# Low parts of the keys stacked over 128 rows in the attention scores of 64-row heads

## The chip, the cores and the metric

One core of one Trainium2 chip runs the whole program in one launch. The metric is the device time of that core in microseconds, as the median of three runs. Engines are named as in the profile: PE is TensorE (its matmuls; PEld its weight loads), DVE is VectorE, ACT is ScalarE, POOL is GpSimd, SP is SyncE, which issues the DMAs.

## The reference

For 512 tokens of width 2048, two hybrid attention layers run one after another, and behind them a block with a pooling branch, a state space branch and a gated embedding. The change lies in the attention of the two layers. Each layer has three branches with causal softmax attention:

```
# differential attention: 4 heads, 2 score maps each, 64 channels per map
s = einsum('bqhcd,bkhcd->bhcqk', q, k) * 64 ** -0.5      # causal mask, softmax
a = p[:, :, 0] - lam * p[:, :, 1]
# sliding window: 16 query heads, 2 key heads of 64 channels, window 128
s = einsum('bnqgrd,bnkgd->bngrqk', q, k_band) * 64 ** -0.5
# latent attention: 4 heads; 128 channels without rotation, 64 rotated, the rotated key shared
s = einsum('bqhd,bkhd->bhqk', concat(q_nope, q_rope), concat(k_nope, k_rope)) * 192 ** -0.5
```

All arrays are float32.

## The kernel before

TensorE works on float32r operands. To keep float32 accuracy every operand is split into a high part (rounded to float32r) and a low part (the rest), and a product is three matmuls into one PSUM bank: high by high, high by low, low by high (`mm3`). A matmul takes stationary weights, loaded into the array (128 rows are the channels that are summed over, 128 columns), and moves up to 512 columns of the other operand through it; every matmul has its own weight load.

The program is a sequence of projections on TensorE (512 output columns over 16 tiles of channels). The weights stream in by DMA in pieces of two units (`wraw`); ScalarE makes the high part (`whi`), VectorE the low part (`wlo`), and a ring keeps four units split ahead of the one in use (`AHEAD`). Between the steps of a projection the attention work of finished heads is placed: `step` counts the TensorE time of the projection, and each 1310 ns of it `tick` lets waiting pieces go on when a small model, kept while the program is written, finds their operands written and their banks free. So each engine has a fixed order, in which attention pieces stand between projection steps. An attention unit has five pieces: scores (TensorE, then the mask and the maximum on VectorE), exp (ScalarE), norm (VectorE), transposes (TensorE, split by ScalarE and VectorE), and probabilities times values (TensorE).

For heads of 64 channels the scores use the 128 rows of the array for two parts at once. `to_stack` takes a rotated [channel, token] tile that holds two heads, one in rows 0 to 63 and one in rows 64 to 127. For queries it makes two tiles `sa` and `sb`, one per head, with the head's high part in one half of the rows and its low part in the other (the half that has to change rows is copied by DMA). For keys of the differential branch it makes `sa` and `sb` with the head's high part in both halves, and one tile `sl` with the low parts of both heads, each in its own half. `mm_stacked` then needs two steps per score map: over 128 rows (high by high and low by high at once), and over the 64 rows in which the head's own high query part lies (high query by low key). The sliding-window keys (`hi`, `lo` from `kd`) and the latent branch's rotated key (`hi`, `lo` from `kr`) have their low part in both halves of the rows already.

In a sliding-window unit (`sw_unit`, 8 per key head and layer) two pairs of heads are worked on, each over 256 key columns, into the banks `s0` and `s1`. In a differential unit (`da_units`) the two score maps of a head go to `s0` and `s1`, over 256, 256, 384 and 512 key columns for the four query tiles. In a latent unit (`mla_units`) one head goes to one bank: three steps of `mm3` for the 128 channels, then the two stacked steps.

In the rows of the trace a matmul is written out<-moving,stationary: `s<-hi,sa` is a score step with key tile `hi` moving and the queries `sa` stationary, `s<-lo,sa` is the step with the low key tile. The helper that records every operation gives all of them line L166, so the rows are told apart by their tiles and shapes: `128*128 128x256` is a full step of 256 columns, `64*128 64x256` a step over 64 rows.

Of the kernel before, what the change touches and what calls it, by code (L numbers as in the profile page):

```python
# [85 lines left out]
class Model:  # L86
    """A rough account, kept while the program is written, of when each engine gets to an instruction and
    each tile is written. Work beside the projections is placed where its operands should be there."""
# [53 lines left out]
    def ready(self, need, eng, banks):  # L142
        """Whether eng would find these tiles written and banks of these tags free."""
        limit = max(self.t[eng], self.t["PE"])
        for tag in set(banks):
            names, bufs = self.held.get(tag, ()), self.bufs.get(tag, 1)
            for i in range(len(names) + banks.count(tag) - bufs):
                if self.used.get(names[i], 0.0) + 130 > limit:
                    return False
        return all(x is not None and self.done.get(x.tensor.name, 1e18) + 130 <= limit for x in need)  # L150
# [5 lines left out]
class Engine:  # L156
    """An engine's instructions, passed on and entered in the model."""
# [24 lines left out]
class Step:  # L182
    """A piece of work that is best begun when eng would find the tiles that need() names written."""
# [9 lines left out]
class K:  # L193
# [87 lines left out]
    def chain(self, fs, gap=1.0, delay=0.0, q=None):  # L281
        """Steps that run one after another, at least gap ticks apart; None leaves a place free, and one
        that returns False is called again later."""
        self.n += 1
        heapq.heappush(self.bg if q is None else q, (self.now + delay + gap, self.n, list(fs), gap))

    def force(self, q):
        """Runs the next step that can be, ready or not."""
        self.run_urgent()
        late, got = [], False  # L290
        while q and not got:
            x = heapq.heappop(q)
            got = self.is_emitted(x[2][0]) and self.run_step(x[2][0]) is not False
            if got:
                self.advance(q, x)
            else:
                late.append(x)
        assert got
        for x in late:
            heapq.heappush(q, x)  # L300
# [17 lines left out]
    def att_start(self, units, ticks, delay=0, done=None):  # L318
        """Units of (scores, exp, norm, transposes, values); one is begun every so many ticks."""
        gap = ticks / len(units)  # L320
        t = self.now + delay
        for x in units:
            self.queue.append([list(x), 0, t])
            t += gap
        if done:
            self.queue[-1][0].append(done)

    def run_units(self, force=False):
        """A unit goes on once the one before it is two parts further."""
        before = 5  # L330
        for x in list(self.queue):
            steps, pos, t = x
            if t > self.now and not force:
                break
            while pos < len(steps) and (before >= min(pos + 2, 5)):
                f = steps[pos]
                if not (self.is_emitted(f) if force else self.is_ready(f)):
                    break
                self.run_step(f)
                pos += 1  # L340
                if force:
                    force = False
                    x[1] = pos
                    if pos == len(steps):
                        self.queue.remove(x)
                    return True
            x[1] = pos
            if pos == len(steps):
                self.queue.remove(x)
                before = 5  # L350
            else:
                before = pos
        return False
# [18 lines left out]
    def rsqrt_list(self, out, ss, scale, eps, n):  # L372
        """Closures that put (ss * scale + eps) ** -0.5 into out[0]."""
# [26 lines left out]
    def rsqrt1(self, ss, scale, eps):  # L400
        """(ss * scale + eps) ** -0.5 of one column; the powers of two that the steps leave are taken out at the end."""
# [18 lines left out]
    def units(self, name):  # L420
        """How many units of up to 512 columns, and the k-tiles and columns of each."""
# [10 lines left out]
    def plan_loads(self):  # L432
        """Pieces of one or two units, and after which split the load of each is issued."""
# [55 lines left out]
    def ahead(self, n=AHEAD):  # L489
        """Keeps n units of the ring split beside the one in use."""  # L490
# [20 lines left out]
    def proj_cm(self, name, mov, ncol, evac, hook=None):  # L511
        """out[channel, token]: the weights stationary."""
# [17 lines left out]
    def proj_tm(self, name, stat, ms, evac, hook=None):  # L530
        """out[token, channel]: the activations stationary."""
# [99 lines left out]
    def reduce_list(self, tiles):  # L631
        """The steps of reduce_angle as closures."""
        return [lambda x=x: self.reduce_angle(*tiles(), part=x) for x in range(4)]

    def reduce_angle(self, a, k, r, part=None):
        """r = a - 2 pi round(a / 2 pi), the multiple taken off in pieces that are exact; in one go or by part."""
# [48 lines left out]
    def norm_list(self, m, xt, after_sq=None, tags="tttt", act=False, first=False):  # L685
        """Closures: x / rms(x), transposed into the columns of token tile m of B."""
# [72 lines left out]
    def rope_lists(self, raws, fins):  # L759
        """Rotates the [channel, token] tiles; fins get each result."""  # L760
# [29 lines left out]
    def to_stack(self, dst, i, keys=False):  # L790
        """Two heads of 64 rows for products whose 128 rows carry both parts: [hi; lo] and [lo; hi] of them, or,
        for keys, [hi; hi] of either, and the two heads' lo."""
        def f(x):
            a, b, lo = (self.u(F32R, name=n) for n in ("sa", "sb", "sl"))
            self.nc.scalar.copy(a, x)
            self.nc.scalar.copy(b[64:128, :], x[64:128, :])
            self.urgent.append(lambda: self.nc.vector.tensor_tensor(out=lo, in0=x, in1=a, op=ALU.subtract))

            def move():
                self.nc.sync.dma_start(a[64:128, :].bitcast(F32), (a if keys else lo)[0:64, :].bitcast(F32))  # L800
                self.nc.sync.dma_start(b[0:64, :].bitcast(F32), (b if keys else lo)[64:128, :].bitcast(F32))
                dst[i] = (a, b, lo) if keys else (a, b)

            self.chain([Step(move, lambda: [lo], "SP")], 0.3)
        return f

    def mm_stacked(self, outs, qs, ks, rows, start=True):
        """hi hi + lo hi over 128 rows, then hi lo over the head's own 64."""
# [3 lines left out]
        for o, q, k, r in zip(outs, qs, ks, rows):  # L812
            nc.tensor.matmul(o, q[r], k[1][r], start=False, stop=True)

# [1 line left out]
    def sw_unit(self, l, g, pp2, i, q, kd, v, yr):  # L816
# [8 lines left out]
        def scores():  # L825
            p, mx = [], self.small(4, name="mx")
            banks = [self.bank(f"s{e}") for e in range(2)]
            for a in range(2):
                self.mm_stacked([b[:, a * 256:(a + 1) * 256] for b in banks],
                                [x[:, i * P:(i + 1) * P] for x in q[2 * pp2 + a]],  # L830
                                [[x[:, k0 * P:k0 * P + 256] for x in kd[g]]] * 2, HALVES)
# [94 lines left out]
    def da_units(self, l, h, qk, va, done):  # L926
        """qk() gives the tiles of q and k; done(o) comes after the last one."""
# [4 lines left out]
        for i in range(NT):  # L932
# [3 lines left out]
            def scores(i=i, st=st):  # L936
# [5 lines left out]
                                [(x[:, :w], k[2][:, :w]) for x in k[:2]], HALVES)  # L942
# [33 lines left out]
    def mla_units(self, h, qk, vc, done):  # L976
# [5 lines left out]
        for i in range(NT):  # L982
# [3 lines left out]
            def scores(i=i, st=st, n=n):  # L986
# [5 lines left out]
                self.mm_stacked([b[:, :w]], [qr[e][:, i * P:(i + 1) * P]], [[x[:, :w] for x in kr]], HALVES[e:e + 1], False)  # L992
# [30 lines left out]
    def cm_norm_list(self, xs, n, eps, cols, after):  # L1023
        """Closures: x * rsqrt(mean over the channels) * column, for [channel, token] tiles, in place."""
# [60 lines left out]
    def plan_tail(self, name, last):  # L1085
        """The last chunk stays on the chip, split; the end of it stays in the ring."""
# [6 lines left out]
    def layer(self, l):  # L1093
# [66 lines left out]
        # sliding window  # L1160
# [44 lines left out]
        # differential attention  # L1205
# [47 lines left out]
        # latent attention, over the last projection and the first chunk of the output projection  # L1253
# [25 lines left out]
        def hook(k0):  # L1279
            """Rows of B that the last projection has passed take the branches' outputs."""  # L1280
# [27 lines left out]
    def tail_rows(self, name, evac):  # L1308
        """The resident last chunk, token tile by token tile."""
# [70 lines left out]
    def cmul(self, dst, a, b, e1, e2, tmp, neg_im=False):  # L1380
        """dst = a * b for (re, im) pairs of views; tmp: two scratch views."""
# [12 lines left out]
    def exp_list(self, get):  # L1394
        """exp of get() = (x, out, k, t), in closures; x, k and t are overwritten."""
# [157 lines left out]
    def cdiag(self, c, pr):  # L1553
        """c of two groups, each in its rows and columns."""
        return self.cd[c][pr // 16][:, pr % 16].rearrange("p e c -> p (e c)")

    def ssm_lists(self, ct, ud, yd, put):
        """Closures of one channel tile (8 groups): its tables, then the scan and its output."""
# [226 lines left out]
    def second(self, xsrc):  # L1785
# [36 lines left out]
        # pooling branch  # L1822
# [84 lines left out]
        # gated linear unit of the state space branch  # L1907
# [29 lines left out]
        # output projection, residual  # L1937
# [49 lines left out]
        # embedding, its gate, final norm  # L1987
# [81 lines left out]
def _layout(inp):  # L2069
# [80 lines left out]
    # constants of the shapes  # L2150
# [35 lines left out]
```

## Time and profile before

| | before |
|---|---|
| median of 3 runs | 2713.55 us (2711.83 to 2714.47) |
| profiled execution, first to last instruction (the page gives no other time for it) | 2711.1 us |
| TensorE busy | 2648.9 us, 13120 matmuls |
| TensorE weight loads busy | 2201.1 us |
| VectorE busy | 1599.1 us |
| ScalarE busy | 1197.8 us |
| GpSimd busy | 415.5 us |

The span is the time from the first to the last instruction in one execution; the median is of other executions and is 2.4 us above it. Busy is the time covered by an engine's instructions; matmuls are pipelined, so that their durations overlap, and the distance from one start to the next tells more than a duration.

### The profile page before, as it was taken

How to read it: one execution, taken by the hardware profiler on the slowest of the kernel's cores; microseconds unless marked ns; L12 is line 12 of the kernel's file. 1: busy time of each engine (PE TensorE's matmuls, PEld its weight loads, DVE VectorE, ACT ScalarE, POOL GpSimd, SP SyncE). 2: the span in 40 equal slices, each digit the busy share in tenths (PEclk: the TensorE clock that was granted, in tenths of full speed). 3: DMA queues.
4: the chain of work that ended last, by engine and by line, in shares of the span. 5: the costliest groups of instructions: out<-in, count | busy, mean ns of one | idle time of the engine just before them, and what ended most of it. 6: DMA issues, size and time to landing. Idle time of an engine off the chain costs nothing. (4 is left out here: it accounts for less than half of the span.)

```text
span 2711.1 us, 36803 instructions
## 1 busy us (share of the span) xinstructions
PE 2648.9 (98%) x13120; PEld 2201.1 (81%) x13120; DVE 1599.1 (59%) x3247; ACT 1197.8 (44%) x2543; POOL 415.5 (15%) x822
## 2 busy tenths in 40 slices
PE   8999999999999999999999999989999999999998
PEld 8978888877888887888777788888877888888886
DVE  6785566675624758546667562486767654333344
ACT  7565444544434646444444443463333343232341
POOL 0100001100001110000110000117777800000000
PEclk9999999999999999999999999999999999999999
DMA  6642333223235553224422323454232332352332
GB/s 213 186 120 86 91 119 113 75 78 125 71 116 163 173 147 94 94 89 122 117 71 79 124 70 117 160 186 141 84 94 82 100 99 94 118 164 69 101 127 91
DMA packets 125831, 309.04 MB, mean 114 GB/s; under 512 B 33616, under 2 KB 34512, under 8 KB 125648
## 3 DMA queue, kind: packets, MB, share of 16 engines
q1 hardware_dynamic: 125648, 306.69, 36.1%
q8 instruction: 103, 1.69, 0.3%
q14 instruction: 80, 0.66, 0.1%
HBM read 264.68 MB, written 20.97 MB: 105 GB/s over the span
## 5 line engine op out<-in xcount | busy, mean ns | idle before, releaser
L166 PE MATMUL pp<-B,whi 128*128 128x512 f32 (+1 forms) x4256 | 1222.6, 373 | 7.5 <-DVE g L166 6.2
L166 PEld LDWEIGHTS pp<-B,whi 128*128 128x128 f32 x4256 | 753.9, 190 | 137.7 <-issue 7.1
L166 PE MATMUL pp<-B,wlo 128*128 128x512 f32 (+1 forms) x2128 | 782.4, 368 | 8.9 <-DVE wlo L166 8.9
L166 PE MATMUL pp<-whi,B 128*128 128x512 f32 x1984 | 626.0, 391 | 1.6 <-ACT raw L166 1.0
L166 DVE SCALAR_TENSOR_TENSOR wlo<-wraw,p_cols,whi 128x512 fp32r<-128x512 f32 (+1 forms) x576 | 448.4, 795 | 293.7 <-ACT whi L166 290.0
L166 ACT ACTIVATE whi<-wraw,p_cols 128x512 fp32r<-128x512 f32 (+1 forms) x576 | 395.9, 713 | 206.8 <-PE pp L166 170.8
L166 PEld LDWEIGHTS pp<-B,wlo 128*128 128x128 f32 x2128 | 403.5, 190 | 78.2 <-DVE wlo L166 10.3
L166 PEld LDWEIGHTS pp<-whi,B 128*128 128x128 f32 x1984 | 372.4, 188 | 82.2 <-ACT raw L166 1.8
L166 DVE TENSOR_TENSOR wlo<-wraw,whi 128x512 fp32r<-128x512 f32 x288 | 197.8, 696 | 386.9 <-ACT whi L166 386.5
L166 PE MATMUL pp<-wlo,B 128*128 128x512 f32 x992 | 386.2, 389 | 0.0
L166 ACT CAST whi<-wraw 128x512 fp32r<-128x512 f32 x288 | 175.5, 623 | 323.4 <-PE pp L166 311.0
L166 PEld LDWEIGHTS pp<-wlo,B 128*128 128x128 f32 x992 | 186.4, 188 | 37.1
L166 POOL TENSOR_TENSOR sw<-sw,sinT 128x512 f32<-128x512 f32 x40 | 55.2, 1386 | 764.7 <-DMA sw<-raw 708.8
L166 POOL TENSOR_TENSOR o<-o,x 128x512 f32<-128x512 f32 x32 | 51.1, 1623 | 378.4 <-DVE o L166 370.4
L166 PE MATMUL pp<-rh,B 128*128 128x512 f32 x320 | 103.1, 392 | 0.0
L166 PE MATMUL pp<-hi,whi 128*128 128x512 f32 x224 | 88.3, 394 | 1.4 <-DVE lo L166 1.4
L166 PE MATMUL pp<-hi,wlo 128*128 128x512 f32 x224 | 87.3, 390 | 0.0
L166 PE MATMUL pp<-lo,whi 128*128 128x512 f32 x224 | 87.3, 390 | 0.0
L166 ACT ACTIVATE p<-p,nb 128x256 f32<-128x256 f32 (+1 forms) x128 | 60.2, 473 | 57.9 <-DVE nb L166 57.8
L166 ACT CAST pth<-t 128x256 fp32r<-128x256 f32 (+1 forms) x96 | 29.2, 339 | 113.2 <-PE t L166 110.5
L166 PEld LDWEIGHTS pp<-rh,B 128*128 128x128 f32 x320 | 60.1, 188 | 12.3
L166 DVE TENSOR_SCALAR p<-p,sm 128x128 f32<-128x128 f32 (+1 forms) x192 | 66.0, 386 | 4.1 <-DVE sm L166 0.5
(257 smaller groups left out, 3162.7 us busy)
## 6 DMA issues: line engine op xcount, KB each, us to landing
wraw<-in_w SPq DMA_DIRECT2D x426, 512.0 KB, 3.5
sw<-raw SPq DMA_DIRECT2D x160, 64.0 KB, 2.0
wraw<-in_w SPq DMA_DIRECT2D x24, 384.0 KB, 3.2
x<-in_x SPq DMA_DIRECT2D x32, 256.0 KB, 5.2
x<-o SPq DMA_DIRECT2D x32, 256.0 KB, 2.6
ybd<-yb SPq DMA_DIRECT2D x16, 256.0 KB, 4.5
yb<-ybd SPq DMA_DIRECT2D x16, 256.0 KB, 3.8
x<-x SPq DMA_DIRECT2D x16, 256.0 KB, 4.4
```

The costliest lines, as they stand in the source:

```text
L166: r = f(*a, **k)
```

## The change

`to_stack` for keys: the low parts of the two heads go to two tiles, `lo` and `lb`, by two subtractions over 64 rows each, and each is copied by DMA to the other half of its rows. `mm_stacked` then takes all 128 rows in the second step too, with the same stationary queries as in the first; the step now adds the product of the two low parts, which was left out before. The two steps of one score map follow each other directly, where before the first steps of both maps came ahead of the second steps. For the sliding window and the latent branch nothing but the rows and the order of the steps changes.

```
     def to_stack(self, dst, i, keys=False):
...
         def f(x):
             a, b, lo = (self.u(F32R, name=n) for n in ("sa", "sb", "sl"))
+            V = self.nc.vector
             self.nc.scalar.copy(a, x)
             self.nc.scalar.copy(b[64:128, :], x[64:128, :])
-            self.urgent.append(lambda: self.nc.vector.tensor_tensor(out=lo, in0=x, in1=a, op=ALU.subtract))
+            if keys:
+                lb = self.u(F32R, name="sl")
+                for d, r in zip((lo, lb), HALVES):
+                    self.urgent.append(lambda d=d, r=r: V.tensor_tensor(out=d[r, :], in0=x[r, :], in1=a[r, :],
+                                                                        op=ALU.subtract))
+            else:
+                self.urgent.append(lambda: V.tensor_tensor(out=lo, in0=x, in1=a, op=ALU.subtract))
 
             def move():
-                self.nc.sync.dma_start(a[64:128, :].bitcast(F32), (a if keys else lo)[0:64, :].bitcast(F32))
-                self.nc.sync.dma_start(b[0:64, :].bitcast(F32), (b if keys else lo)[64:128, :].bitcast(F32))
-                dst[i] = (a, b, lo) if keys else (a, b)
-
-            self.chain([Step(move, lambda: [lo], "SP")], 0.3)
+                dup = [(a, a if keys else lo, 0), (b, b if keys else lo, 1)] + ([(lo, lo, 0), (lb, lb, 1)] if keys else [])
+                for d, s, h in dup:
+                    self.nc.sync.dma_start(d[HALVES[1 - h], :].bitcast(F32), s[HALVES[h], :].bitcast(F32))
+                dst[i] = (a, b, lo, lb) if keys else (a, b)
+
+            self.chain([Step(move, lambda: [lo, lb] if keys else [lo], "SP")], 0.3)
         return f
 
-    def mm_stacked(self, outs, qs, ks, rows, start=True):
+    def mm_stacked(self, outs, qs, ks, start=True):
         nc = self.nc
         for o, q, k in zip(outs, qs, ks):
             nc.tensor.matmul(o, q, k[0], start=start, stop=False)
-        for o, q, k, r in zip(outs, qs, ks, rows):
-            nc.tensor.matmul(o, q[r], k[1][r], start=False, stop=True)
+            nc.tensor.matmul(o, q, k[1], start=False, stop=True)
...
-                                [[x[:, k0 * P:k0 * P + 256] for x in kd[g]]] * 2, HALVES)
+                                [[x[:, k0 * P:k0 * P + 256] for x in kd[g]]] * 2)
...
-                                [(x[:, :w], k[2][:, :w]) for x in k[:2]], HALVES)
+                                [[x[:, :w] for x in k[e::2]] for e in range(2)])
...
-                self.mm_stacked([b[:, :w]], [qr[e][:, i * P:(i + 1) * P]], [[x[:, :w] for x in kr]], HALVES[e:e + 1], False)
+                self.mm_stacked([b[:, :w]], [qr[e][:, i * P:(i + 1) * P]], [[x[:, :w] for x in kr]], False)
```

On TensorE, in the first sliding-window unit of layer one, the difference of the two programs reads as follows (`s_1779` and `s_1780` are the two score banks, `hi_1690` and `lo_1691` the keys, `sa` and `sb` the queries of the two heads of a pair; the shape is that of the columns written, so that a step over 64 rows reads as 128x256 too):

```order
 L166 MATMUL s_1779<-hi_1690,sa_1561 128x256
+L166 MATMUL s_1779<-lo_1691,sa_1561 128x256
 L166 MATMUL s_1780<-hi_1690,sb_1562 128x256
-L166 MATMUL s_1779<-lo_1691,sa_1561 128x256
 L166 MATMUL s_1780<-lo_1691,sb_1562 128x256
 L166 MATMUL s_1779<-hi_1690,sa_1612 128x256
+L166 MATMUL s_1779<-lo_1691,sa_1612 128x256
 L166 MATMUL s_1780<-hi_1690,sb_1613 128x256
-L166 MATMUL s_1779<-lo_1691,sa_1612 128x256
 L166 MATMUL s_1780<-lo_1691,sb_1613 128x256
```

Each low step moved up by one place, behind the high step into the same bank; the number of steps is the same.

On SP, where the first two key tiles of the differential branch in layer one are moved, the queue has before the change (64x512 are copies between halves of rows, `wraw` the loads of weights):

```order
L166 DMA sa_3768<-sl_3770 64x512
L166 DMA sb_3769<-sl_3770 64x512
L166 DMA wraw_3830<-in_w 128x1024
L166 DMA sa_3806<-sa_3806 64x512
L166 DMA sb_3807<-sb_3807 64x512
L166 DMA wraw_3873<-in_w 128x1024
L166 DMA sa_3841<-sa_3841 64x512
L166 DMA sb_3842<-sb_3842 64x512
L166 DMA wraw_3950<-in_w 128x1024
```

and after it:

```order
L166 DMA sb_3769<-sl_3770 64x512
L166 DMA wraw_3832<-in_w 128x1024
L166 DMA sa_3806<-sa_3806 64x512
L166 DMA sb_3807<-sb_3807 64x512
L166 DMA sl_3808<-sl_3808 64x512
L166 DMA sl_3811<-sl_3811 64x512
L166 DMA wraw_3879<-in_w 128x1024
L166 DMA sa_3845<-sa_3845 64x512
L166 DMA sb_3846<-sb_3846 64x512
L166 DMA sl_3847<-sl_3847 64x512
L166 DMA sl_3850<-sl_3850 64x512
```

Two copies of a low tile stand ahead of the next load of weights that was behind the tile's two other copies before.

## Rows read from the trace of the kernel before

**Rows 1.** The page: span, busy time and share of two engines, granted clock by slices.

```profile
span 2711.1 us, 36803 instructions
PE 2648.9 (98%) x13120; PEld 2201.1 (81%) x13120; DVE 1599.1 (59%) x3247; ACT 1197.8 (44%) x2543; POOL 415.5 (15%) x822
PEclk9999999999999999999999999999999999999999
```

**Rows 2.** Waits of TensorE, whole run: us in total, times, longest.

```profile
PE t L166 <- DVE p L166: 5.0, 5, 1.8
```

**Rows 3.** Timeline of PE, first sliding-window unit: start us, duration us, engine, line, operation, tiles.

```profile
138.65 0.28 PE L166 MATMUL s<-hi,sa 128*128 128x256 f32 x1
138.76 0.28 PE L166 MATMUL s<-hi,sb 128*128 128x256 f32 x1
138.98 0.38 PE L166 MATMUL s<-lo,sa 64*128 64x256 f32 x1
138.98 0.38 PE L166 MATMUL s<-lo,sb 64*128 64x256 f32 x1
139.29 0.38 PE L166 MATMUL s<-hi,sa 128*128 128x256 f32 x1
139.51 0.28 PE L166 MATMUL s<-hi,sb 128*128 128x256 f32 x1
...
140.03 0.73 PE L166 MATMUL pp<-B,whi 128*128 128x512 f32 x2
140.60 0.40 PE L166 MATMUL pp<-B,wlo 128*128 128x512 f32 x1
140.83 0.62 PE L166 MATMUL pp<-B,whi 128*128 128x512 f32 x2
141.29 0.39 PE L166 MATMUL pp<-B,wlo 128*128 128x512 f32 x1
```

**Rows 4.** Timeline of PE, a differential unit of 512 key columns.

```profile
426.12 0.39 PE L166 MATMUL s<-sa,sa 128*128 128x512 f32 x1
426.35 0.39 PE L166 MATMUL s<-sb,sb 128*128 128x512 f32 x1
426.67 0.50 PE L166 MATMUL s<-sl,sa 64*128 64x512 f32 x1
...
427.10 0.73 PE L166 MATMUL pp<-B,whi 128*128 128x512 f32 x2
```

**Rows 5.** Timeline of PE, end of a latent unit of 256 key columns.

```profile
643.65 0.28 PE L166 MATMUL s<-hi,lo 128*128 128x256 f32 x1
643.76 0.28 PE L166 MATMUL s<-hi,sa 128*128 128x256 f32 x1
643.97 0.38 PE L166 MATMUL s<-lo,sa 64*128 64x256 f32 x1
644.28 0.72 PE L166 MATMUL pp<-B,whi 128*128 128x512 f32 x2
```

**Rows 6.** Timeline of PE, probabilities times values of a differential head, full steps only.

```profile
407.39 0.28 PE L166 MATMUL t<-pth,hi 128*128 128x256 f32 x1
...
407.99 0.28 PE L166 MATMUL t<-pth,lo 128*128 128x256 f32 x1
408.11 0.63 PE L166 MATMUL pp<-B,whi 128*128 128x512 f32 x2
408.58 0.39 PE L166 MATMUL pp<-B,wlo 128*128 128x512 f32 x1
```

**Rows 7.** Steps on query tile sa: ns min/median/max, first and last start us, forms.

```profile
L166 PE MATMUL s<-lo,sa x80: 379/381/498, 139.0 to 1582.4; 64*128 64x256 f32 x72, 64*128 64x384 f32 x4, 64*128 64x512 f32 x4
L166 PE MATMUL s<-sl,sa x32: 379/408/500, 389.4 to 1462.7; 64*128 64x256 f32 x16, 64*128 64x384 f32 x8, 64*128 64x512 f32 x8
```

**Rows 8.** Tile sa: the subtractions that read it, and SP's issue of its copies.

```profile
L166 DVE TENSOR_TENSOR sl<-raw,sa x36: 682/692/1809, 114.6 to 1510.4; 128x512 fp32r<-128x512 f32 x36
L166 SPq DMA_DIRECT2D sa<-sa x8: 461/462/467, 358.2 to 1344.4; - x8
```

**Rows 9.** DMA issues: tiles, count, KB each, us from issue to landing.

```profile
sa<-sa SPq DMA_DIRECT2D x8, 128.0 KB, 4.3
```

## Prediction

> **What bounds the kernel now.** I read the page first. TensorE is busy 98% of the span of 2711.1 us, at full granted clock in all 40 slices [rows 1]: 2.4 GHz, the upper of its two levels. VectorE has 59% [rows 1]. A busy share of 98% says only that matmul durations cover the span; they overlap (a matmul of 512 columns lasts 0.39 us and its follower starts 0.23 us after it), so it does not say that the array streams all that time. Hence the second view, the waits. Over the whole run TensorE's transposes wait five times for VectorE's probabilities, 5.0 us together [rows 2], and span less busy time leaves 62 us without any work. A stage that shortens TensorE's own stream therefore shortens the run almost one for one, if the waits do not grow.
>
> The third view is what the change is about: the timeline of TensorE inside one score block, read by the distance from one start to the next. In a sliding-window unit [rows 3] two 128-row score steps start 0.11 us apart (138.65, 138.76). The first 64-row step starts 0.22 us after that, and the second one at the same instant (both 138.98): the two halves of the array work side by side. Then nothing starts for 0.31 us. The next 128-row step (139.29) is itself followed only after 0.22 us, and after the second group the first pair of projection steps takes 0.57 us to the next row (140.03 to 140.60) where it takes 0.46 us undisturbed (140.83 to 141.29). So around every group of 64-row steps the stream loses time three times: on entering, on leaving, and on the first full step after it. None of it is called idle, since earlier matmuls' durations cover it.
>
> **What the change removes, per block.** All low steps become 128-row steps. The price of a 128-row step of 256 columns in a run of them, each with its own weight load, is 0.12 us: six probability-times-value steps take 0.72 us from 407.39 to 408.11, and the projection pair behind them takes 0.47 us, so nothing is lost on leaving [rows 6]. In the latent block before its 64-row step two such steps follow each other after 0.11 us (643.65, 643.76) [rows 5].
>
> - Sliding window. From the first score step at 138.65 to the row at 140.60, less the 0.46 us that its pair of projection steps takes anyway, is 1.49 us for eight steps [rows 3]. Eight full steps at 0.12 us are 0.96 us. Saved: 0.53 us a unit. There are 32 units (2 layers, 2 key groups, 2 pairs of heads, 4 query tiles), with two groups each: 64 of the 80 64-row steps with queries sa and a low key tile lo [rows 7]. 32 x 0.53 = 17.0 us.
> - Differential attention, 32 groups, one per pair of score maps (the 64-row steps with key tile sl [rows 7]). At 256 columns (16 of them) a group is half of the sliding-window unit, 0.745 us, against 4 x 0.12 = 0.48: 0.265 us, 4.2 us together. At 512 columns (8) it lasts from 426.12 to 427.10 and costs the 0.11 us behind it, 1.09 us [rows 4]; four full steps at 0.23 us, the distance between 426.12 and 426.35, are 0.92 us: saved 0.17 us, 1.4 us together. The eight at 384 columns lie between, 0.22 us each, 1.7 us.
> - Latent attention, 32 blocks, where a single 64-row step has no partner (2 layers, 4 heads, 4 query tiles: the other 16 of those 80 on sa [rows 7], and as many on sb). From 643.76 to 644.28 plus 0.11 us is 0.63 us for two steps [rows 5]; two full ones are 0.24 us. Saved 0.39 us; the wider blocks lose the same three pieces, so 32 x 0.39 = 12.5 us.
>
> Sum: 17.0 + 4.2 + 1.4 + 1.7 + 12.5 = 36.8 us. The full step's price is the value on which this hangs. With 0.11 us in place of 0.12 us the sum is 19.5 + 4.9 + 3.1 + 13.1 = 40.6 us, which is the upper end. The trace has no run of two 128-row steps with the same queries and two key tiles into one score bank; the nearest rows are the two just named, of the same shape, and I see no wait that could stand between. If the three losses belonged to the score banks and not to the 64-row form, nothing would be saved, which is the lower end (a rival below).
>
> **What it adds.** Per key tile one more subtraction on VectorE (the two heads' low parts go to two tiles, each over 64 rows) and two more copies of 64 rows by DMA; one more buffer of the pool of 48. There are 8 key tiles. The subtraction of 128 rows takes 0.692 us [rows 8]; half the rows could cost anything from half of that to all of it, and I take all: 8 x 0.69 = 5.5 us of VectorE, which is 59% busy, so hidden; without that cover it would be 5.5 us. A copy is 0.46 us on SP's queue [rows 8] and lands 4.3 us after issue [rows 9]. Two more copies put the weight load queued behind them back by about 1 us, eight times; the weights are split four units ahead of a unit that keeps TensorE 12 x 0.23 = 2.7 us busy, so this is covered too (8 us if it were not). The copies themselves are issued from 358.2 [rows 8] and the first step that needs them starts at 389.4 [rows 7]: some 20 us to spare after two more copies and the landing. The order of the work beside the projections moves by a few places only; the score steps of a pair change places, which costs nothing of its own.
>
> **What becomes late next.** TensorE reaches its transposes sooner by what the score blocks between save. Where it waits for probabilities already (five times [rows 2]) the saving of one block, at most 0.39 us, goes into the wait: about 2 us. I take 36.8 - 1.8 = 35 us. From the span of 2711.1 us this leaves 2676.1; the median of the runs shown, 2713.55, is 2.4 us above the span, and I leave that as it is: **2678.5 us**.
>
> **A rule against the row.** The Trainium skill, page "TensorE: Matmul & The Clock Gate", section "Why this matters for your kernels", says that small-K matmuls in distinct row groups run concurrently, and that a matmul of few rows alone takes the time of one with 128. By it a pair of 64-row steps costs one step's time, and the change would lose; it holds here for the starts (both 138.98) but not for what surrounds them. The page "TensorEngine Tiling (Array Packing)", section "Key Properties", has the other half: changing the tiling mode drains TensorE. The trace agrees with that one: 0.22 us going in, 0.31 us coming out.
>
> **Rivals.**
> - *Slower: packing lost, gaps kept.* If the losses come from switching the score bank after an unfinished accumulation, they stay, and the 80 pairs of 256 columns and 16 wider ones each pay one more step: 80 x 0.12 + 8 x 0.175 (between 0.12 and 0.23) + 8 x 0.23 = 12.8 us, 2726 us. For it: banks do alternate in the sliding-window rows. Against it: in the latent block the 64-row step follows a full one into the same bank, with the same queries, and the gap of 0.21 us is there all the same [rows 5]. It decides as soon as full steps of a block start over 0.19 us apart. Chance 3%.
> - *Part given back to waits.* In latent attention TensorE gets from scores to transposes 0.39 us sooner, and VectorE and ScalarE do not get faster. If each differential and latent block lost its saving in a wait, 4.2 + 1.4 + 1.7 + 12.5 = 19.8 us would go, and the time would be about 2696. Against it: only five such waits now. Chance 14%, from 2687 to 2705.
> - *No change.* TensorE's saving would have to be taken whole by the supply of split weights, TensorE waiting for the low parts instead: 2713. Against it: VectorE has 41% of the span free. Chance 4%.
> - *The forecast*, 2670 to 2686 (the two prices of a full step, with the waits at nothing to 5 us): 79%.
>
> **How the numbers follow.** The likeliest case gives 2678.5. The range of 80% takes the forecast's and the start of the second rival: 2670 to 2692. A change under 0.2% (5.4 us) cannot be told from none. Faster by more: 0.79 + 0.14 = 0.93; within: 0.04; slower: 0.03.
>
> **What would show it.** In the changed profile no matmul of 64 rows is left; eight steps of a sliding-window unit start 0.11 to 0.12 us apart; the projection pair behind them takes 0.46 us and not 0.57; the start-to-start sum over a latent block falls by 0.39 us. TensorE's busy time falls by about as much as the span, since the gaps counted as busy. The prediction is wrong if full steps on the DMA-filled key tiles start further apart than 0.12 us, if the waits for probabilities grow from 5 us to more than some 10 us, or if TensorE waits at the first differential block for a copy.

## The result and the profile after

The changed kernel takes 2680.95 us (median of 4 runs, 2678.94 to 2681.69) where the kernel before takes 2712.69 us beside it: a ratio of 0.9883, 95% interval 0.9872 to 0.9895, or 31.7 us less. Forecast were 2678.5 us and a gain of 35 us.

The page of the changed kernel, the same lines as [rows 1]:

```profile
span 2676.9 us, 36843 instructions
PE 2609.8 (97%) x13120; PEld 2198.8 (82%) x13120; DVE 1603.1 (60%) x3255; ACT 1198.4 (45%) x2543; POOL 414.0 (15%) x822
PEclk9999999999999999999999999999999999999999
```

The span is 34.2 us shorter. TensorE's busy time fell by 39.1 us although it issues the same 13120 matmuls, and the rest of the span, without work on TensorE, grew from 62.2 to 67.1 us. VectorE has the eight subtractions more. The profiled execution is the fastest of the four; its mean granted clock is 0.995, that of the profile before 0.993, both close under the upper level of 2.4 GHz. The changed kernel was profiled once more (in the run beside the old order, below), at 0.993:

```profile
span 2678.8 us, 36843 instructions
PE 2611.8 (97%) x13120; PEld 2199.9 (82%) x13120; DVE 1603.5 (60%) x3255; ACT 1199.1 (45%) x2543; POOL 414.4 (15%) x822
```

Here the span is 32.3 us shorter than before, near the 31.7 us of the medians, TensorE's busy time 37.1 us less, and the rest of the span 67.0 us.

The timeline of TensorE in the first sliding-window unit, which answers to [rows 3] (start us, duration us):

```profile
138.59 0.28 PE L166 MATMUL s<-hi,sa 128*128 128x256 f32 x1
138.70 0.28 PE L166 MATMUL s<-lo,sa 128*128 128x256 f32 x1
138.82 0.28 PE L166 MATMUL s<-hi,sb 128*128 128x256 f32 x1
...
139.42 0.28 PE L166 MATMUL s<-lo,sb 128*128 128x256 f32 x1
139.54 0.63 PE L166 MATMUL pp<-B,whi 128*128 128x512 f32 x2
140.01 0.39 PE L166 MATMUL pp<-B,wlo 128*128 128x512 f32 x1
```

Eight steps start 0.11 to 0.12 us apart, and the projection pair behind them takes 0.47 us (139.54 to 140.01), not 0.57. By the way of counting that gave 1.49 us before, the unit now takes 140.01 - 0.46 - 138.59 = 0.96 us, to the hundredth the value that the prediction put for it. A differential unit of 512 columns, which answers to [rows 4], goes from 426.12 to 427.10 before, and now:

```profile
420.54 0.39 PE L166 MATMUL s<-sa,sa 128*128 128x512 f32 x1
420.77 0.39 PE L166 MATMUL s<-sl,sa 128*128 128x512 f32 x1
420.99 0.39 PE L166 MATMUL s<-sb,sb 128*128 128x512 f32 x1
421.22 0.39 PE L166 MATMUL s<-sl,sb 128*128 128x512 f32 x1
421.45 0.62 PE L166 MATMUL pp<-B,whi 128*128 128x512 f32 x2
```

That is 0.91 us for four full steps; the prediction put 0.92. The two low tiles that were partly filled by DMA are streamed at the price of any other tile: 0.22 to 0.23 us to the next step.

Among the waits of TensorE over the whole run (us in total, times, longest), the line of [rows 2]:

```profile
...
PE t L166 <- DVE p L166: 5.9, 8, 1.7
...
```

The waits for probabilities are 5.9 us in eight places, where they were 5.0 us in five. The first differential scores, at 384.05 us, start 0.12 us apart and wait for no copy.

### The profile page after: what moved, and what is told of

Its sections match the earlier page's. It is cut to its first block, busy times and chain, and to the rows that moved or that the text cites. A ratio compares the mean times of both kernels' runs of the same rounds, so it can differ in the third digit from the quotient of the medians.

```text
span 2676.9 us, 36843 instructions
## 1 busy us (share of the span) xinstructions
PE 2609.8 (97%) x13120; PEld 2198.8 (82%) x13120; DVE 1603.1 (60%) x3255; ACT 1198.4 (45%) x2543; POOL 414.0 (15%) x822
## 3 DMA queue, kind: packets, MB, share of 16 engines
q1 hardware_dynamic: 126928, 308.79, 37.1%
## 5 line engine op out<-in xcount | busy, mean ns | idle before, releaser
L166 ACT ACTIVATE p<-s,mx 128x128 f32<-128x128 f32 (+3 forms) x96 | 50.6, 530 | 46.5 <-DVE mx L166 44.5
```

The lines of the kernel that those rows point to most:

```text
L166: r = f(*a, **k)
```

## The experiments

My theory: a group of 64-row steps between 128-row steps (an excursion into the 64-row form) costs TensorE a fixed time, for entering the form and for leaving it, whatever the group holds, and this was what the change took away. The rivals: the order of the steps and the score banks; the number of 64-row steps; and the additions (copies, subtractions, a buffer), which might cost something that hides a larger gain.

**Full steps in the old order** (all steps over 128 rows, but both high steps of a pair ahead of both low ones):

```
-            nc.tensor.matmul(o, q, k[1], start=False, stop=True)
+        for o, q, k in zip(outs, qs, ks):
+            nc.tensor.matmul(o, q, k[1], start=False, stop=True)
```

> All steps over 128 rows as in the change, but in the order of before (both high steps of a pair, then both low steps). If the gain comes from leaving the 64-row form, this is the changed kernel again: 2681 us, within 4 us. If it comes from the two steps of a score map following each other into one bank, half of the gain or more goes: 2697 us or above. In the trace the eight steps of a sliding-window unit would then start further apart than 0.12 us.

2678.34 us, ratio 0.9876 (0.9863 to 0.9890). Run again beside the changed kernel on one chip:

> The changed kernel once more, beside the next one on the same chip, since its median (2681.0) stands 2.6 us above that of the same steps in the old order (2678.3). If the order of the two steps has no price of its own, the two agree within 2 us, at 2678 to 2681 us.

> All steps over 128 rows in the old order, once more. If the order of the change (same bank twice running) costs something, this one stays 2 to 3 us below the changed kernel; if not, they agree within 2 us.

2680.65 us for the changed kernel, ratio 0.9886 (0.9869 to 0.9902), and 2679.49 us for the old order, 0.9881 (0.9867 to 0.9896). They cannot be told apart; the order of the steps has no price that shows, as long as all are over 128 rows.

**Half steps without a partner** (the kernel before; each low step right behind its high step):

```
-        for o, q, k in zip(outs, qs, ks):
-            nc.tensor.matmul(o, q, k[0], start=start, stop=False)
         for o, q, k, r in zip(outs, qs, ks, rows):
+            nc.tensor.matmul(o, q, k[0], start=start, stop=False)
             nc.tensor.matmul(o, q[r], k[1][r], start=False, stop=True)
```

> The kernel before (64-row low steps, no added copies) in the order of the change: each low step follows its own high step, so that no two 64-row steps are neighbours and each makes an entering and a leaving of its own. Leaving the 64-row form as the cause: a high and a low step alone cost 0.63 us at 256 columns [rows 5], so a sliding-window unit 2.52 us in place of 1.49, 32 x 1.03 = 33 us; differential pairs 16 x 0.52 + 8 x 0.57 + 8 x 0.63 = 18 us; about 2763 us. If only the work side by side of two neighbours is lost, one step for each of 96 pairs, about 13 us: 2726 us. If the order makes the gain: 2697 us or below.

2759.39 us against 2712.37, ratio 1.0175 (1.0161 to 1.0189): 47.0 us slower, where leaving the 64-row form as the cause had put 51 us (33 + 18). The timeline of TensorE in its first sliding-window unit:

```profile
139.32 0.28 PE L166 MATMUL s<-hi,sa 128*128 128x256 f32 x1
139.52 0.38 PE L166 MATMUL s<-lo,sa 64*128 64x256 f32 x1
139.84 0.38 PE L166 MATMUL s<-hi,sb 128*128 128x256 f32 x1
140.15 0.38 PE L166 MATMUL s<-lo,sb 64*128 64x256 f32 x1
...
141.71 0.73 PE L166 MATMUL pp<-B,whi 128*128 128x512 f32 x2
```

The first 64-row step starts 0.20 us after the full step ahead of it; from there on every step from one form to the other takes 0.31 us, in both directions. In the changed kernel's unit the same tiles, banks and order give 0.12 us; only the rows differ. (Elsewhere this edit also moved some attention pieces by a few places in the engines' order.) Over the whole run the median differential pair, with the three TensorE steps behind it, grew by 0.51 us at 256 columns and by 0.63 us at 512. The 0.12 us between the two is about what a step of 512 columns costs above one of 256 (0.23 against 0.12 us), which fits a loss of one step's time when two neighbours no longer run side by side.

**One excursion in place of two** (the kernel before; in a sliding-window unit the second pair of heads takes its low steps first, so that the four 64-row steps of the unit stand together):

```
-                                [[x[:, k0 * P:k0 * P + 256] for x in kd[g]]] * 2, HALVES)
+                                [[x[:, k0 * P:k0 * P + 256] for x in kd[g]]] * 2, HALVES, low_first=a == 1)
...
+        for x, part in enumerate((low, high) if low_first else (high, low)):
+            for o, q, k in part:
+                nc.tensor.matmul(o, q, k, start=start and x == 0, stop=x == 1)
```

> The kernel before, the differential and latent branches untouched; in a sliding-window unit the second pair of heads takes its low steps first, so that the unit has four full steps outside and the four 64-row steps in one piece between them: one entering and one leaving of the 64-row form in place of two, with the same steps. If the loss is per change of form, a unit costs 0.11 + 0.21 + x + 0.31 + 0.22 + 0.11 = 0.96 us + x in place of 1.49, where x, the distance of two 64-row pairs, is not in any row: between 0.12 (loads ahead) and 0.31 us (no loads ahead). 32 units save 7 to 13 us: 2700 to 2706 us. If the loss is per 64-row step, nothing changes: 2712.7 us.

2701.66 us against 2712.47, ratio 0.9961 (0.9949 to 0.9974): 10.8 us saved with the same steps, so the price is per excursion and not per step. Its first unit in the timeline of TensorE:

```profile
138.46 0.27 PE L166 MATMUL s<-hi,sa 128*128 128x256 f32 x1
138.57 0.28 PE L166 MATMUL s<-hi,sb 128*128 128x256 f32 x1
138.78 0.38 PE L166 MATMUL s<-lo,sa 64*128 64x256 f32 x1
138.78 0.39 PE L166 MATMUL s<-lo,sb 64*128 64x256 f32 x1
139.00 0.28 PE L166 MATMUL s<-lo,sa 64*128 64x256 f32 x1
139.00 0.28 PE L166 MATMUL s<-lo,sb 64*128 64x256 f32 x1
139.21 0.39 PE L166 MATMUL s<-hi,sa 128*128 128x256 f32 x1
139.44 0.28 PE L166 MATMUL s<-hi,sb 128*128 128x256 f32 x1
139.55 0.64 PE L166 MATMUL pp<-B,whi 128*128 128x512 f32 x2
140.03 0.39 PE L166 MATMUL pp<-B,wlo 128*128 128x512 f32 x1
```

and its weight loads there:

```profile
138.46 0.19 PEld L166 LDWEIGHTS s<-hi,sb 128*128 128x128 f32 x1
138.78 0.18 PEld L166 LDWEIGHTS s<-lo,sa 64*128 64x128 f32 x1
...
138.88 0.19 PEld L166 LDWEIGHTS s<-lo,sa 64*128 64x128 f32 x1
...
139.21 0.19 PEld L166 LDWEIGHTS s<-hi,sa 128*128 128x128 f32 x1
```

The unit takes 140.03 - 0.46 - 138.46 = 1.11 us where it took 1.49. The starts show where an excursion loses its time. A full step normally has its load begun ahead (138.46 for the step at 138.57). At a change of form the load starts with the step (138.78 and 138.78; 139.21 and 139.21): it lies open, and that costs some 0.10 us, seen as a step of 0.22 us to the next (138.78 to 139.00, 139.21 to 139.44) where 0.11 to 0.12 us is the rule. And the change itself takes another 0.10 us each way (138.57 to 138.78, 139.00 to 139.21, with some 0.11 us of streaming in each). Two changes and two open loads make about 0.4 us; this split is read from the starts, and no run varies the two parts by themselves. The second pair of 64-row steps has its load begun ahead (138.88 for 139.00), so inside the form no further load lies open. The value of x that the rows before did not show is 0.22 us, and the first pair's open load is in it. The way out takes 0.21 us (139.00 to 139.21) and not the 0.31 us that the expectation put: in the kernel before that open load was part of the 0.31 us, so the expectation counts it twice. The Trainium skill, "TensorEngine Tiling (Array Packing)", section "Key Properties", says that a change of tiling mode, and not a change of tile, drains TensorE. The trace agrees with that difference: about 0.4 us around the group, and nothing between its two pairs beyond the first pair's open load.

**The latent branch alone** (the kernel before, one edit):

```
-                self.mm_stacked([b[:, :w]], [qr[e][:, i * P:(i + 1) * P]], [[x[:, :w] for x in kr]], HALVES[e:e + 1], False)
+                self.mm_stacked([b[:, :w]], [qr[e][:, i * P:(i + 1) * P]], [[x[:, :w] for x in kr]], [slice(0, P)], False)
```

> Full low steps in the latent branch alone; no other edit, the same order on every engine. A 64-row step has no partner there, so a rule of concurrency expects no change: 2712.7 us. By the rows 32 blocks lose 0.39 us each: 12.5 us, 2700 us, or some 2 us above if waits for the probabilities take a part.

2699.71 us, ratio 0.9956 (0.9942 to 0.9969): 12.8 us, with 32 steps widened from 64 to 128 rows and no instruction added, removed or moved. The block that answers to [rows 5]:

```profile
643.10 0.28 PE L166 MATMUL s<-hi,lo 128*128 128x256 f32 x1
643.21 0.28 PE L166 MATMUL s<-hi,sa 128*128 128x256 f32 x1
643.33 0.28 PE L166 MATMUL s<-lo,sa 128*128 128x256 f32 x1
643.45 0.63 PE L166 MATMUL pp<-B,whi 128*128 128x512 f32 x2
643.92 0.39 PE L166 MATMUL pp<-B,wlo 128*128 128x512 f32 x1
```

From 643.21 to 643.45 are 0.24 us for the two stacked steps, and the pair behind them takes 0.47 us.

**The differential branch left** (full steps in the other two branches; the edit above and, in the sliding-window unit):

```
-                                [[x[:, k0 * P:k0 * P + 256] for x in kd[g]]] * 2, HALVES)
+                                [[x[:, k0 * P:k0 * P + 256] for x in kd[g]]] * 2, [slice(0, P)] * 2)
```

> Full steps in the sliding-window and latent branches alone, whose key tiles have the low part in both halves already; the differential branch as before, so no copy, subtraction or buffer is added. By my sum these parts hold 17.0 + 12.5 of 36.8 us; with the measured gain of 31.7 us in the same proportion 25 us, so 2687 us (2684 to 2691). If the added copies and subtractions cost what they would uncovered (5 to 13 us), leaving them out makes this as fast as the changed kernel or faster: 2681 us or below.

2686.23 us, ratio 0.9902 (0.9887 to 0.9917). So the sliding window is worth about 2699.71 - 2686.23 = 13.5 us, and the differential branch with all that is added for it 2686.23 - 2680.95 = 5.3 us; each difference of two medians may be off by some 2 us. The three other runs with all steps over 128 rows (2680.65, 2679.49 and 2678.34 us) put the differential branch at 5.6, 6.7 and 7.9 us.

**The additions alone** (the kernel before with the new `to_stack`; the score steps stay over 64 rows):

```
-                                [(x[:, :w], k[2][:, :w]) for x in k[:2]], HALVES)
+                                [[x[:, :w] for x in k[e::2]] for e in range(2)], HALVES)
```

> The kernel before with the additions alone: the second low tile, the two subtractions over 64 rows and the four copies of each differential key tile are made, but all low steps stay over 64 rows in the old order. If the additions are hidden: 2712.7 us, within 3 us. If VectorE's or SP's time for them shows: 2718 to 2726 us.

2712.38 us against 2712.37, ratio 1.0000 (0.9991 to 1.0009). They do not show. The sixteen subtractions, in the changed kernel (groups by shape on VectorE):

```profile
L166 DVE TENSOR_TENSOR sl<-raw,sa 64x512 fp32r<-64x512 f32 x16 | 11.0, 686 | 4.8 <-ACT sa L166 4.6
```

A subtraction over 64 rows takes 0.686 us, as much as one over 128 (0.692 us [rows 8]); the sixteen copies of low tiles land 4.2 us after their issue.

## Why the prediction was right

**The mechanism and the place** were as forecast. The number of excursions ties the runs together. The kernel before has 64 of them in sliding-window units, 32 in differential and 32 in latent blocks: 128. The run without partners has 96 more; it is 47.0 us slower, of which by the prediction's sum 12.8 us (an estimate) are steps that no longer run side by side, which leaves 34.2 / 96 = 0.36 us each. The run with one excursion per unit has 32 fewer: 10.8 / 32 = 0.34 us. The latent run has 32 fewer: 12.8 / 32 = 0.40 us. The change has 128 fewer and pays 12.8 us for work that ran side by side: (31.7 + 12.8) / 128 = 0.35 us.

**The terms of the sum.** By the medians: latent 12.5 us forecast, 12.8 measured; differential 7.3 forecast, 5.3 to 7.9 measured; sliding window 17.0 forecast, 13.5 measured. The blocks themselves shrank as forecast in all three. Added up over the two traces, from the first stacked step of each block (`mm_stacked`) to the start of the third TensorE step behind the block, they take 16.4 us less in the sliding window, 7.4 us in the differential and 12.4 us in the latent branch: 36.2 us of the 36.8 forecast.

The term that was mis-sized is the one for what becomes late next: 1.8 us were put for the growth of TensorE's waits, and the time without work on TensorE grew by 4.9 us, from 62.2 to 67.1. 36.2 - 4.9 = 31.3 us is close to the 31.7 us of the medians. The step behind the term was wrong too: it let the five waits for probabilities take up the saving, and these grew by 0.9 us only. Most of the growth came in the sliding window. In the run with the differential branch left, which has the order of before on every engine, the waits between the first sliding-window and the first differential scores are, in the first layer:

```profile
PE pp L166 <- DVE g L166: 0.7, 1, 0.7
PE s L166 <- DVE p L166: 0.6, 1, 0.6
PE pp L166 <- ACT raw L166: 0.5, 1, 0.5
PE t L166 <- ACT yb L166: 0.2, 1, 0.2
```

and in the second layer:

```profile
PE t L166 <- DVE lo L166: 1.9, 2, 1.8
PE t L166 <- ACT yb L166: 0.8, 1, 0.8
PE pp L166 <- ACT raw L166: 0.5, 1, 0.5
```

This is 5.2 us. The same stretches of the kernel before hold 2.8 us, in the first layer

```profile
PE pp L166 <- DVE g L166: 0.5, 1, 0.5
PE pp L166 <- ACT raw L166: 0.5, 1, 0.5
```

and in the second:

```profile
PE t L166 <- DVE lo L166: 1.0, 2, 0.9
PE pp L166 <- ACT raw L166: 0.5, 1, 0.5
PE t L166 <- ACT yb L166: 0.3, 1, 0.3
```

TensorE runs into VectorE and ScalarE there by 2.4 us more. This is no scatter of one execution. In the same two stretches the two other kernels with the old units (latent alone, additions alone) wait 2.8 and 2.7 us and the run without partners, whose units are longer, 2.4 us; all six profiles with shorter units have 4.8 to 6.4 us. In the changed kernel it is 6.4 us, 3.6 of the 4.9 us; why each single wait grew was not followed.

**The range.** The two prices of a full step and waits of nothing to 5 us give 2673 to 2682 us, not the 2670 to 2686 us that stand for the forecast; for the 3 to 4 us more on each side no reason is given. The measured time, 2680.95 us, lies in both.

**What was costed at nothing** cost nothing: the additions alone move the time by 0.0 us (at most 2.4 us by the interval).

**The rivals.** Packing lost and gaps kept: the gaps are gone with the form, and the order of banks has no price that shows. Part given back to waits: 4.9 us went, not 19.8. The Trainium skill, "TensorE: Matmul & The Clock Gate", section "Why this matters for your kernels", says that small-K matmuls in distinct row groups run concurrently. The trace agrees for the starts (both 138.98 in [rows 3]). The time that this saves is given up by the change, 12.8 us by the prediction's sum; it is less than the some 45 us (31.7 + 12.8) of the excursions.

## What to carry to other kernels

Read a tuned TensorE stream by the distance from start to start, not by busy time or idle time: some 45 us of 2712 lay in gaps that the page counted as work. Two 64-row matmuls side by side save one step (0.12 us at 256 columns, 0.23 at 512), but a group of them between full steps costs about 0.35 to 0.4 us here. By these numbers, as an estimate, packing pays only from three or four pairs in a group at 256 columns and from two at 512. The most that ran here, two pairs of 256 columns, still lose: 1.11 us for the unit against 0.96 us with full steps. For one pair or a single step it was cheaper to fill the unused rows with a harmless term. When TensorE is the bound and a block in it shrinks, count a few microseconds for the waits that the next engines then show, in all places and not only where they wait already.

## What was not expected of the hardware

That the loss, as read from the starts, splits so evenly: some 0.10 us for each change of form and 0.10 us for the first weight load after each, which is not begun ahead, while loads inside either form are. And that the subtraction over 64 rows costs 0.686 us against 0.692 us over 128 [rows 8]: at the same 512 columns, half the rows saved nothing.
